# Gated half v of a gated MLP by seven products of block sums, with sums of weight blocks made in the transfers

## Chip, core and metric

The kernel runs on one core of one Trainium2 chip. The metric is the device time of one execution in microseconds (us); the profile has one execution of its own, whose span is the time from its first to its last instruction. TensorE multiplies, VectorE (DVE) and ScalarE (ACT) do elementwise work, GpSimd (POOL) a little of it, SyncE (SP) issues most transfers.

## Reference

One sample of 512 tokens with 1024 features passes two layers, each with a token mixer and a squared-ReLU MLP, all in float32. The change touches the mixer of layer 1:

```python
def spatial_gating(h, w_in, b_in, ln_g, ln_b, w_s, b_s, w_o):
    z = jax.nn.gelu(h @ w_in + b_in, approximate=False)      # w_in (1024, 6144)
    u, v = jnp.split(z, 2, axis=-1)                          # 3072 columns each
    v = layer_norm(v, ln_g, ln_b)
    v = v.reshape(bsz, n // SG_CHUNK, SG_CHUNK, SG_GROUPS, SG_GROUP_CH)
    s = jnp.einsum('gpq,bnqgc->bnpgc', w_s, v) + b_s.T[None, None, :, :, None]
    return (u * s.reshape(bsz, n, SG_HALF)) @ w_o
```

"The gated half v" is the product of h (512 x 1024) with the second 3072 columns of `w_in`, with its bias and Gelu.

## The kernel before

**Products.** Each float32 product is made of three passes in float32r: an operand is kept as a rounded part hi and a rest lo, and `products` (L183) issues hi*hi, hi*lo and lo*hi, each a matmul of 128x128 against 128x512 (or narrower). PSUM tiles come from banks named ps_mm, ps_t, ps_o and ps_s.

**Weights.** All weight pieces lie side by side in DRAM (`wall`), in the order of use. The class `Weights` streams them: SP loads a unit of 1536 columns into one of two buffers `raw` (L66), then `upto` splits it in four pieces of 384 columns, whi by a cast on ACT (L80) and wlo by a subtraction on DVE (L81). `get` asks for pieces two units ahead, so the split of a unit is issued ahead of its use. Every fourth pair of tiles lies in a pool of its own, `W.more`.

**Order.** A scheduler has put the instructions of each engine into one order; an engine runs its row strictly in that order, each instruction waiting for what it needs.

**Stages.** Layer 0 is attention and its output projection; then MLP "a". An MLP has two halves of 2048 hidden units: 16 blocks of products, each ended by `hidden` (L562 to L567: relu on ACT, square on DVE, split), then the second matrix in `residual` (L512 adds into `xall`). Between the blocks of MLP "a" stand the steps of `ada_block`, 56 in all: SP loads 512 KB into the only buffer `adaraw` (L276), and DVE reduces it (L277), one value of the modulation of layer 1 for each partition; the next load waits until DVE has read the one before.

At the end of MLP "a" the last two output blocks are done by token halves, and for each half `Norm.finish` (L156 to L159) and `modulated` (L167 to L174) make the next input, h_hi (hh) and h_lo (hl), eight chunks k of 128 features: on DVE, ACT and POOL, half 0 while PE still works on half 1.

Then comes the stage that is changed: for 6 blocks b of 512 columns and 4 tiles n of 128 tokens, 8 chunks k in three passes, 576 matmuls in all, in which tokens are the stationary operand and the weights move. A finished tile is taken from PSUM by DVE (L616, adding the bias), goes through Gelu on ACT (L617) and statistics on DVE (L618). After it the half u is computed by blocks, layer norm runs over v (L620 to L635), and L656 mixes positions.

Of the kernel before, what the change touches and what calls it, by code (L numbers as in the profile page):

```python
# [27 lines left out]
UNIT = 1536  # L28
# [9 lines left out]
# The weight stream: sections of pieces in the order of their use, (name, pieces, columns of a piece).  # L38
# [8 lines left out]

class Weights:
    """Streams of stationary or moving weight pieces, split into two float32r parts on arrival."""

    def __init__(self, nc, raw_pool, pool, wall, ahead=2):
        self.nc, self.raw_pool, self.pool, self.ahead, self.wall = nc, raw_pool, pool, ahead, wall
        self.first, self.width = {}, {}
        c = 0
        for key, n, w in SECTIONS:
            self.first[key], self.width[key] = c, w
            c += n * w
        self.tiles = {}
        self.raw = {}
        self.loaded = self.done = 0  # L60
        self.more, self.parts = None, 4
# [8 lines left out]
    def upto(self, unit):  # L70
        nc = self.nc
        while self.done <= min(unit, self.wall.shape[0] - 1):
            self.load(self.done)
            raw = self.raw.pop(self.done)
            pool = self.more if self.more is not None and self.done % 4 == 3 else self.pool
            hi = pool.tile([P, UNIT], F32R, tag="whi", name="whi")
            lo = pool.tile([P, UNIT], F32R, tag="wlo", name="wlo")
            for c in range(0, UNIT, UNIT // self.parts):
                cs = slice(c, c + UNIT // self.parts)
                nc.scalar.copy(out=hi[:, cs], in_=raw[:, cs])  # L80
                nc.vector.tensor_tensor(out=lo[:, cs], in0=raw[:, cs], in1=hi[:, cs], op=ALU.subtract)  # L81
            self.tiles[self.done] = (hi, lo)
            self.done += 1

    def get(self, key, i):
        w = self.width[key]
        u, c = divmod(self.first[key] + i * w, UNIT)
        assert c + w <= UNIT
        self.upto(u + self.ahead - 1)
        hi, lo = self.tiles[u]  # L90
# [4 lines left out]
def backbone_kernel(ctx: ExitStack, tc: tile.TileContext, x0T, xT, cols, ada0, ada1, qknorm, bias_t,  # L95
# [38 lines left out]
    h_hi = [hp.tile([P, T], F32R, tag=f"hh{k}", name=f"hh{k}") for k in range(KC)]  # L134
    h_lo = [hp.tile([P, T], F32R, tag=f"hl{k}", name=f"hl{k}") for k in range(KC)]
# [247 lines left out]
    def both(kk, j):  # L383
        """Columns of the grid keys of query block j and of the context keys, as one pattern."""
# [98 lines left out]
    W.more = ctx.enter_context(tc.tile_pool(name="wb", bufs=1, reuse_waits="tile"))  # L483
# [293 lines left out]
```

## Time and profile before

| | us |
|---|---|
| median of three runs | 1563.95 (1559.7 to 1568.19) |
| the profiled execution, its span | 1560.2 |
| PE busy | 1524.9 (98%) |
| DVE busy | 930.1 (60%) |
| ACT busy | 664.3 (43%) |
| POOL busy | 148.8 (10%) |

The profiled execution has no time of its own beside its span; the span lies within the three runs, 3.75 us below their median. Busy PE includes the time of matmuls at a lower clock. The shares are means over stages, and what a stage waits for is read from that stage.

### The profile page before, as it was taken

Reading aid. Unit: us, or ns where it says so; the run is one execution under the profiler, and the core shown is the slowest. Engines: PE = TensorE matmul, PEld = TensorE weight load, DVE = VectorE, ACT = ScalarE, POOL = GpSimd, SP = SyncE. Lnnn points to the kernel's source line nnn. Section 1 sums busy time; section 2 is a strip of 40 time slices with the busy share of each in tenths; the row PEclk is TensorE's granted clock in tenths of the full one; section 3 lists DMA queues with packets and bytes.
Section 4 is the critical chain, followed back from the end, with each engine's and each line's share of the span. In section 5 each row is a group of like instructions: output and inputs, shape, how many; then the busy total and the mean of one; then the engine's idle time right before and its main releaser. Section 6 shows DMA issues by size and latency. Waiting matters only on the chain.

```text
span 1560.2 us, 21105 instructions
## 1 busy us (share of the span) xinstructions
PE 1524.9 (98%) x7780; PEld 1287.6 (83%) x7780; DVE 930.1 (60%) x1938; ACT 664.3 (43%) x1577; POOL 148.8 (10%) x177
## 2 busy tenths in 40 slices
PE   8899999999999999999999999999999999999999
PEld 2798888887898888878988887888889988888888
DVE  5778777777776555765575468644446743334431
ACT  2566666676544322442353256423234542224320
POOL 0522222212200000000100013100001000000000
PEclk9999999999999999999999999999999999999999
DMA  9265555535146555655243225322321432223230
GB/s 354 95 171 174 164 163 167 167 113 167 62 142 211 193 193 180 202 199 179 95 128 131 91 96 176 125 92 97 106 95 41 135 109 87 96 101 102 97 112 28
DMA packets 60311, 212.06 MB, mean 136 GB/s; under 512 B 7984, under 2 KB 16816, under 8 KB 58672
## 3 DMA queue, kind: packets, MB, share of 16 engines
q1 hardware_dynamic: 48688, 200.57, 39.2%
q10 hardware_dynamic: 11520, 10.15, 2.1%
q8 instruction: 61, 1.00, 0.3%
q14 instruction: 42, 0.34, 0.1%
HBM read 193.91 MB, written 2.10 MB: 126 GB/s over the span
## 4 chain that ended last, share of the span: by engine, by line
PE 59%; DMA 8%; DVE 4%; issue 2%; ACT 1%; ACTq 0%; DVEq 0%
PE ps_mm L183 29%; PE ps_t L183 19%; PE ps_o L183 9%; DMA adaraw<-ada 8%; DVE adaraw L277 1%; PE ps_s L656 1%; DVE wlo L81 1%; DVE nt L172 1%; DVE hl L174 0%; DVE xall L512 0%; DMA raw<-wall 0%; PE ps_s L156 0%; ACT v L632 0%; DVE acc L151 0%; ACT whi L80 0%
## 5 line engine op out<-in xcount | busy, mean ns | idle before, releaser
L80 ACT CAST whi<-raw 128x384 fp32r<-128x384 f32 x620 | 278.5, 510 | 355.9 <-PE ps_mm L183 141.5
L81 DVE TENSOR_TENSOR wlo<-raw,whi 128x384 fp32r<-128x384 f32 x620 | 330.6, 581 | 144.8 <-ACT whi L80 144.6
L277 DVE CUSTOM_DVE_ANT_0 adaraw<-adaraw,cb 128x1024 f32<-128x1024 f32 x80 | 99.4, 1242 | 106.6 <-DMA adaraw<-ada 106.1
L183 PE MATMUL ps_mm<-hh,wlo 128*128 128x512 f32 (+1 forms) x416 | 154.2, 371 | 0.6 <-DVE wlo L81 0.6
L183 PE MATMUL ps_mm<-hh,whi 128*128 128x512 f32 (+1 forms) x416 | 154.4, 371 | 0.0
L183 PE MATMUL ps_mm<-hl,whi 128*128 128x512 f32 (+1 forms) x416 | 154.0, 370 | 0.0
L183 PE MATMUL ps_mm<-whi,hh 128*128 128x384 f32 (+1 forms) x352 | 124.7, 356 | 5.1 <-DVE vl L332 2.9
L183 PE MATMUL ps_mm<-wlo,hh 128*128 128x384 f32 (+1 forms) x352 | 124.8, 355 | 1.9 <-DVE wlo L81 1.9
L183 PE MATMUL ps_mm<-mh,whi 128*128 128x512 f32 (+1 forms) x336 | 122.0, 363 | 3.2 <-ACT mh L566 3.2
L183 PE MATMUL ps_mm<-whi,hl 128*128 128x384 f32 (+1 forms) x352 | 124.1, 354 | 0.0
L183 PE MATMUL ps_mm<-ml,whi 128*128 128x512 f32 (+1 forms) x336 | 122.1, 363 | 0.0
L183 PE MATMUL ps_mm<-mh,wlo 128*128 128x512 f32 (+1 forms) x336 | 121.6, 362 | 0.0
L183 PE MATMUL ps_t<-hh,whi 128*128 128x512 f32 (+1 forms) x280 | 104.5, 373 | 0.0
L183 PE MATMUL ps_t<-hl,whi 128*128 128x512 f32 (+1 forms) x280 | 104.3, 372 | 0.0
L183 PE MATMUL ps_t<-hh,wlo 128*128 128x512 f32 (+1 forms) x280 | 104.0, 371 | 0.0
L183 PEld LDWEIGHTS ps_mm<-hh,wlo 128*128 128x128 f32 x416 | 78.5, 189 | 13.8 <-DVE wlo L81 0.8
L183 PEld LDWEIGHTS ps_mm<-hh,whi 128*128 128x128 f32 x416 | 78.5, 189 | 12.6
L183 PEld LDWEIGHTS ps_mm<-hl,whi 128*128 128x128 f32 x416 | 78.6, 189 | 12.5
L566 ACT CAST mh<-relu 128x512 fp32r<-128x512 f32 x64 | 39.7, 621 | 99.0 <-DVE relu L563 99.0
L183 PEld LDWEIGHTS ps_mm<-mh,whi 128*128 128x128 f32 x336 | 64.2, 191 | 13.1 <-ACT mh L566 3.6
L183 PEld LDWEIGHTS ps_mm<-whi,hh 128*128 128x128 f32 x352 | 66.6, 189 | 10.2 <-DVE vl L332 3.2
L183 PEld LDWEIGHTS ps_mm<-wlo,hh 128*128 128x128 f32 x352 | 66.8, 190 | 7.5 <-DVE wlo L81 2.8
(204 smaller groups left out, 3322.5 us busy)
## 6 DMA issues: line engine op xcount, KB each, us to landing
raw<-wall SPq DMA_DIRECT2D x155, 768.0 KB, 4.4
adaraw<-ada SPq DMA_DIRECT2D x80, 512.0 KB, 3.9
bt<-bias_t SPq DMA_DIRECT2D x16, 512.0 KB, 3.6
aw<-ada SPq DMA_DIRECT2D x7, 1024.0 KB, 10.8
q<-th SPq DMA_DIRECT2D x32, 128.0 KB, 2.4
q<-tl SPq DMA_DIRECT2D x32, 128.0 KB, 2.3
x<-x0T SPq DMA_DIRECT2D x3, 1024.0 KB, 11.3
bc<-lngb ACTq DMA_DIRECT2D x12, 256.0 KB, 3.3
```

Source lines behind the costliest of these rows:

```text
L80: nc.scalar.copy(out=hi[:, cs], in_=raw[:, cs])
L81: nc.vector.tensor_tensor(out=lo[:, cs], in0=raw[:, cs], in1=hi[:, cs], op=ALU.subtract)
L172: vec.scalar_tensor_tensor(out=t, in0=xk, scalar=A[:, k:k + 1], in1=r, op0=ALU.mult, op1=ALU.mult)
L183: pe.matmul(o, lhsT=a, rhs=b, start=start and i == 0, stop=stop and i == n - 1)
L277: vec.tensor_tensor_reduce(out=a, in0=a, in1=cb, scale=1.0, scalar=0.0, op0=ALU.mult, op1=ALU.add, accum_out=mod[:, idx:idx + 1])
L566: act.copy(out=a, in_=r)
L656: pe.matmul(s[:, n * P:(n + 1) * P], lhsT=v[:, n, g * P:(g + 1) * P], rhs=ws, start=True, stop=True)
```

## The change

The two token halves and the two halves of the features form four blocks of h, here B11, B12 (features 0 to 511, token half 0 and 1), B21 and B22 (features 512 to 1023). A pair of column blocks of 512 and the two halves of the features form four blocks of weights, w00, w10 (first columns), w01 and w11. The plain way takes eight products of blocks; the change takes seven, of sums of blocks. It runs for three units u of 1024 columns, each with seven products of 24 matmuls (4 chunks, 2 token tiles, 3 passes), so 504 matmuls in place of 576.

What is added for it:
- Ahead of the first unit, DVE adds hh and hl again to float32 for the four blocks (f, L681), makes T1 = B11-B12, T3 = B22-B12, T2 and T4 from them (L686, L688), and ACT and DVE split each T into hi and lo (L691, L692), all as instructions of 128x1024.
- A sum of weight blocks is made by a plain load from SP (L110), and then a transfer issued by GpSimd that adds a second block (L113), each of 512 KB. The sums w01+w11 lie in two buffers `sum0` and `sum1` and are carried on: a further block is added for n6 and for n3, while n7 and n4 have sums or blocks of their own in `raw`. There are 24 such accumulating transfers, 8 in each unit, beside 10 plain loads of a unit; GpSimd issues them between its own elementwise work.
- Weights to split for this half are now 43008 columns in place of 24576, since each of the seven products has operands of its own.
- PSUM tiles are taken 14 times in a unit, 42 in all, in place of 24 (L726, L729), since a product goes into up to two outputs; Gelu and the statistics keep their 24.

Beside it: `wall` has rows of 2048 columns, `raw` is three buffers of 1024 columns in place of two of 1536, and a split piece is 512 columns in place of 384, for the whole kernel. The pool `W.more` is closed for the changed stage and opened again after it.

The core of the diff:

```diff
+PRODUCTS = (("n1", "B11"), ("n2", "B21"), ("n5", "T1"), ("n6", "T2"), ("n7", "T3"), ("n3", "B22"), ("n4", "T4"))
+def summands(blocks):
+    w00, w01, w10, w11 = blocks
+    return ((False, (w00,)), (False, (w10,)), (None, (w01, w11)), (True, (w00,)), (False, (w00, w01)),
+            (True, (w10,)), (False, (w11,)))
...
-    def load(self, unit):
-        while self.loaded <= min(unit, self.wall.shape[0] - 1):
-            raw = self.raw_pool.tile([P, UNIT], F32, tag="raw", bufs=2, name="raw")
-            self.nc.sync.dma_start(out=raw, in_=self.wall[self.loaded])
...
+            slot, go_on, what = self.stretches[self.loaded]
+            if go_on:
+                raw = self.sums[slot]
+            elif slot is None:
+                raw = self.raw_pool.tile([P, RAW], F32, tag="raw", bufs=3, name="raw")
+            else:
+                raw = self.sums[slot] = self.sum_pool.tile([P, RAW], F32, tag=f"sum{slot}", name=f"sum{slot}")
+            if not go_on:
+                self.nc.sync.dma_start(out=raw, in_=self.dram(what[0], RAW))
+                what = what[1:]
+            for c in what:
+                self.nc.gpsimd.dma_start(out=raw, in_=self.dram(c, RAW), accum_op=ALU.add)
...
-        for b in range(6):
-            w = [W.get("v", b * KC + k) for k in range(KC)]
...
-            for n in range(4):
-                ns = slice(n * P, (n + 1) * P)
-                o = mm()
-                products(o, [((h_hi[k][:, ns], h_lo[k][:, ns]), w[k]) for k in range(KC)], True, True)
-                vs = v[:, n, b * 512:(b + 1) * 512]
-                vec.tensor_tensor(out=vs, in0=o, in1=bb, op=ALU.add)
...
+            for q, (ks, ts) in quarter.items():
+                f[q] = vp.tile([P, HK, HT], F32, tag="f" + q, name="f" + q)
+                vec.tensor_tensor(out=f[q], in0=hh_all[:, ks, ts], in1=hl_all[:, ks, ts], op=ALU.add)
...
+            def operands():
+                operand("T1", f["B11"], f["B12"], False, f["B11"])
+                operand("T3", f["B22"], f["B12"], False, f["B12"])
+                operand("T2", f["B11"], f["B22"], True, f["B22"])
+                operand("T4", f["B22"], f["B21"], True, f["B21"])
...
+                X = [bank("mm", 3) for _ in range(2)]
+                Y = [bank("t", 2) for _ in range(2)]
+                Z = [bank("s", 2) for _ in range(2)]
+                into = {"n1": X, "n2": Y, "n5": Z, "n6": X, "n7": X, "n3": Z, "n4": X}
+                for j, (name, q) in enumerate(PRODUCTS):
+                    hi, lo = ops[q]
+                    o = into[name]
+                    for k in range(HK):
+                        w = W.get("v", (u * 7 + j) * HK + k)
+                        for i in range(2):
+                            ts = slice(i * P, (i + 1) * P)
+                            products(o[i], [((hi[:, k, ts], lo[:, k, ts]), w)],
...
```

Three places of the order follow, in which the names carry the numbers of their buffers. The first is DVE's row where the norm of token half 1 ends (hl is its last result). Before, evacuations of PSUM (L616) and statistics (L618) stand between the parts of hl, and weights (L81) behind:

```order
L172 SCALAR_TENSOR_TENSOR nt_7803<-xall_4516,A1_1_83,rstd_7774 128x256 [waits DVE_49]
L618 BN_STATS st1_7819<-v_7817 128x6 [waits Activation_49]
L174 SCALAR_TENSOR_TENSOR hl6_101<-nt_7803,mod_80,hh6_93 128x256 [waits Activation_49]
L170 TENSOR_TENSOR hl7_102<-nt_7807,hh7_94 128x256 [waits Activation_49]
L616 TENSOR_TENSOR v_7817<-ps_t_7918,bc_7860 128x512 [waits PE_49]
L618 BN_STATS st2_7820<-v_7817 128x6 [waits Activation_49]
L81 TENSOR_TENSOR wlo_7977<-raw_7974,whi_7976 128x384 [waits DMAHW2_49,Activation_49]
```

Now the operands stand there, and ahead of them nothing of the stage v; the first sum's wlo and n1's evacuations stand among them:

```order
L681 TENSOR_TENSOR fB22_7760<-hh_87,hl_88 128x1024 [waits DVE_49]
L688 TENSOR_TENSOR fB11_7754<-fB11_7754,fB12_7756 128x1024 [waits DVE_49]
L729 TENSOR_TENSOR v_7744<-ps_mm_7785,bb_7782 128x512 [waits DMAHW3_49,PE_49]
L688 TENSOR_TENSOR fB12_7756<-fB22_7760,fB12_7756 128x1024 [waits DVE_49]
L692 TENSOR_TENSOR T1l_7764<-fB11_7754,T1h_7763 128x1024 [waits Activation_49]
L686 SCALAR_TENSOR_TENSOR fB22_7760<-fB11_7754,fB22_7760 128x1024 [waits DVE_49]
L692 TENSOR_TENSOR T3l_7769<-fB12_7756,T3h_7768 128x1024 [waits Activation_49]
L686 SCALAR_TENSOR_TENSOR fB21_7758<-fB22_7760,fB21_7758 128x1024 [waits DVE_49]
L692 TENSOR_TENSOR T2l_7774<-fB22_7760,T2h_7773 128x1024 [waits Activation_49,Pool_49]
L124 TENSOR_TENSOR wlo_7822<-sum0_7827,whi_7821 128x512 [waits DMASW2_49]
L692 TENSOR_TENSOR T4l_7779<-fB21_7758,T4h_7778 128x1024 [waits Activation_49]
L729 TENSOR_TENSOR v_7744<-ps_mm_7786,bb_7782 128x512 [waits PE_49]
```

Ahead of the first of these twelve stand, behind the last hl, fB11, fB12 and fB21; behind the last stand the other three pieces of wlo for n5. So eleven instructions of 128x1024 and one evacuation stand between the last hl and the piece of wlo for n5's first chunk or among its follow-ups.

The second place is PE's row after the first 48 matmuls of the stage. Before, the third token tile of the first column block stands there, whose operands are those of half 1's norm:

```order
L183 MATMUL ps_t_7918<-whi_7512,hh0_87 128x512 [waits Activation_49]
L183 MATMUL ps_t_7918<-wlo_7513,hh0_87 128x512
L183 MATMUL ps_t_7918<-whi_7512,hl0_95 128x512 [waits DVE_49]
L183 MATMUL ps_t_7918<-whi_7512,hh1_88 128x512 [waits Activation_49]
L183 MATMUL ps_t_7918<-wlo_7513,hh1_88 128x512
```

Now n5 stands there, behind n1 and n2, which use token half 0 alone; its operands are T1 and the first sum:

```order
L239 MATMUL ps_s_7789<-whi_7821,T1h_7763 128x512 [waits Activation_49]
L239 MATMUL ps_s_7790<-whi_7821,T1h_7763 128x512
L239 MATMUL ps_s_7789<-wlo_7822,T1h_7763 128x512 [waits DVE_49]
L239 MATMUL ps_s_7789<-whi_7821,T1l_7764 128x512
L239 MATMUL ps_s_7790<-wlo_7822,T1h_7763 128x512
L239 MATMUL ps_s_7790<-whi_7821,T1l_7764 128x512
L239 MATMUL ps_s_7789<-whi_7852,T1h_7763 128x512 [waits Activation_49]
L239 MATMUL ps_s_7789<-wlo_7853,T1h_7763 128x512 [waits DVE_49]
```

The third place is DVE's row within a unit: before, splits of loaded weights and evacuations alternate:

```order
L81 TENSOR_TENSOR wlo_7989<-raw_7986,whi_7988 128x384 [waits DMAHW7_49,Activation_49]
L81 TENSOR_TENSOR wlo_7989<-raw_7986,whi_7988 128x384 [waits Activation_49]
L616 TENSOR_TENSOR v_7817<-ps_o_7946,bc_7860 128x512 [waits PE_49]
L81 TENSOR_TENSOR wlo_7989<-raw_7986,whi_7988 128x384 [waits Activation_49] x2
L618 BN_STATS st3_7821<-v_7817 128x6 [waits Activation_49]
```

Now, in the first unit, the split of a sum that waits for an accumulating transfer (the semaphores DMASW) stands ahead of the two evacuations of n6, which free the banks that n7 uses next; and that transfer itself waits for the splits that read the same buffer for n6:

```order
L124 TENSOR_TENSOR wlo_7918<-raw_7921,whi_7917 128x512 [waits Activation_49]
L124 TENSOR_TENSOR wlo_7950<-raw_7946,whi_7949 128x512 [waits DMASW1_49,DVE_49,Activation_49]
L124 TENSOR_TENSOR wlo_7950<-raw_7946,whi_7949 128x512 [waits Activation_49]
L124 TENSOR_TENSOR wlo_7950<-sum0_7827,whi_7949 128x512 [waits DMASW6_49,Activation_49]
L729 TENSOR_TENSOR v_7744<-ps_mm_7785,bb_7782 128x512 [waits PE_49]
L729 TENSOR_TENSOR v_7744<-ps_mm_7786,bb_7782 128x512 [waits PE_49]
```

In the second unit the splits of both sums for n3 stand ahead of n6's evacuations. One thing moves outside of the stage: in MLP "a", counting the steps of `ada_block` in DVE's row, the square for the last hidden block of its second half now stands behind the 74th of them, before behind the 71st.

## Rows read from the trace of the kernel before

**Rows 1.** The page: busy us (share of the span) and instructions

```profile
PE 1524.9 (98%) x7780; PEld 1287.6 (83%) x7780; DVE 930.1 (60%) x1938; ACT 664.3 (43%) x1577; POOL 148.8 (10%) x177
```

**Rows 2.** The page's chain that ended last, by line

```profile
PE ps_mm L183 29%; PE ps_t L183 19%; PE ps_o L183 9%; DMA adaraw<-ada 8%; DVE adaraw L277 1%; PE ps_s L656 1%; DVE wlo L81 1%; DVE nt L172 1%; DVE hl L174 0%; DVE xall L512 0%; DMA raw<-wall 0%; PE ps_s L156 0%; ACT v L632 0%; DVE acc L151 0%; ACT whi L80 0%
```

**Rows 3.** Timeline of PE: start us, us, what, [idle before <-releaser]

```profile
700.30 0.80 PE L183 MATMUL ps_mm<-mh,whi 128*128 128x512 f32 x1 [3.17 <-ACT mh L566]
...
782.37 0.40 PE L183 MATMUL ps_mm<-whi,hh 128*128 128x512 f32 x1
...
786.50 0.70 PE L156 MATMUL ps_s<-acc,ones 128*128 128x256 f32 x2 [1.00 <-DVE acc L151]
...
914.69 0.39 PE L183 MATMUL ps_mm<-hh,whi 128*128 128x512 f32 x1
```

**Rows 4.** Windows: us, busy (x) by engine, PEclk, DMA share, GB/s

```profile
850.00:860.00 10.00, 10.00 (x46) 8.29 (x45) 4.77 (x9) 3.02 (x6) 0.00 (x0) 1.00 0.69 249
790.00:915.00 125.00, 125.00 (x553) 103.55 (x552) 66.46 (x122) 46.34 (x95) 2.39 (x3) 1.00 0.32 103
```

**Rows 5.** Timeline of DVE at the norm of token half 1

```profile
787.81 1.75 DVE L159 RECIPROCAL rstd<-rstd 128x256 f32<-128x256 f32 x1
...
791.17 0.68 DVE L616 TENSOR_TENSOR v<-ps_mm,bc 128x512 f32<-128x512 f32 x1
...
798.76 0.42 DVE L170 TENSOR_TENSOR hl<-nt,hh 128x256 fp32r<-128x256 f32 x1
```

**Rows 6.** Lines by shape: busy us, mean ns, idle before

```profile
L81 DVE TENSOR_TENSOR wlo<-raw,whi 128x384 fp32r<-128x384 f32 x620 | 330.6, 581 | 144.8 <-ACT whi L80 144.6
...
L566 ACT CAST mh<-relu 128x512 fp32r<-128x512 f32 x64 | 39.7, 621 | 99.0 <-DVE relu L563 99.0
...
L169 ACT CAST hh<-nt 128x256 fp32r<-128x256 f32 x18 | 7.0, 389 | 0.0
```

**Rows 7.** Instructions of L634: duration ns min/median/max

```profile
L634 DVE TENSOR_TENSOR v<-v,bc x12: 1211/1224/3022, 921.1 to 983.7; 128x1024 f32<-128x1024 f32 x12
```

**Rows 8.** Windows after PE's wait for mh, columns as in group 4

```profile
700.00:705.00 5.00, 4.70 (x10) 3.43 (x11) 2.19 (x4) 1.90 (x5) 0.00 (x0) 0.50 0.43 144
705.00:710.00 5.00, 5.00 (x20) 4.04 (x19) 3.42 (x9) 0.00 (x0) 0.00 (x0) 0.85 0.76 234
710.00:715.00 5.00, 5.00 (x24) 4.14 (x23) 2.30 (x5) 2.28 (x5) 0.00 (x0) 1.00 0.37 138
```

**Rows 9.** Timeline of DVE: two steps of ada_block

```profile
449.70 1.22 DVE L277 CUSTOM_DVE_ANT_0 adaraw<-adaraw,cb 128x1024 f32<-128x1024 f32 x1
...
697.76 1.22 DVE L277 CUSTOM_DVE_ANT_0 adaraw<-adaraw,cb 128x1024 f32<-128x1024 f32 x1 [0.64 <-DMA adaraw<-ada]
```

**Rows 10.** DMA issues: tile, queue, count, KB each, median us to landing

```profile
raw<-wall SPq DMA_DIRECT2D x155, 768.0 KB, 4.4
adaraw<-ada SPq DMA_DIRECT2D x80, 512.0 KB, 3.9
...
xall<-xT SPq DMA_DIRECT2D x2, 1024.0 KB, 6.5
```

**Rows 11.** Transfers into adaraw

```profile
DMA to landing us min/median/max: 3.3/3.9/10.2
```

**Rows 12.** Timelines of DVE and POOL after the stage v

```profile
926.33 1.49 DVE L662 TENSOR_TENSOR u<-u,gt 128x512 f32<-128x512 f32 x1
...
929.13 0.69 DVE L662 TENSOR_TENSOR u<-u,gt 128x512 f32<-128x512 f32 x1
...
932.23 2.73 DVE L81 TENSOR_TENSOR wlo<-raw,whi 128x384 fp32r<-128x384 f32 x1
...
924.90 2.37 POOL L635 TENSOR_TENSOR v<-v,bc 128x1024 f32<-128x1024 f32 x1 [127.61 <-PE ps_s L656]
```

**Rows 13.** Timeline of DVE: the last evacuation of v

```profile
915.36 0.68 DVE L616 TENSOR_TENSOR v<-ps_mm,bc 128x512 f32<-128x512 f32 x1
```

**Rows 14.** Matmuls of L656: ns min/median/max, first and last start

```profile
L656 PE MATMUL ps_s<-ws,v x192: 270/275/347, 924.4 to 1169.8; 128*128 128x128 f32 x192
```

More of the change, by code (lines that the diff above doesn't have):

```diff
@@ L27 @@
 EPS = 1e-6
-UNIT = 1536
+UNIT = 2048
+RAW = 1024
+PART = 512
+HILO = 1536
 KOFF = (0, 1, 3, 4)
@@ L57, in __init__, with dram @@
             c += n * w
-        self.tiles = {}
-        self.raw = {}
+        self.raw, self.tiles, self.sums = {}, {}, {}
         self.loaded = self.done = 0
-        self.more, self.parts = None, 4
-    def load(self, unit):
-        while self.loaded <= min(unit, self.wall.shape[0] - 1):
-            raw = self.raw_pool.tile([P, UNIT], F32, tag="raw", bufs=2, name="raw")
-            self.nc.sync.dma_start(out=raw, in_=self.wall[self.loaded])
+        self.more = self.sum_pool = None
+    def dram(self, c, n):
+        u, c = divmod(c, UNIT)
+        assert c + n <= UNIT
+        return self.wall[u][:, c:c + n]
@@ L67, in load, with pair @@
             self.raw[self.loaded] = raw
             self.loaded += 1
-    def upto(self, unit):
-        nc = self.nc
-        while self.done <= min(unit, self.wall.shape[0] - 1):
-            self.load(self.done)
[L74 to L82, printed above, removed]
+    def pair(self, n):
+        pool = self.more if self.more is not None and n % 4 == 3 else self.pool
+        return (pool.tile([P, HILO], F32R, tag="whi", name="whi"),
+                pool.tile([P, HILO], F32R, tag="wlo", name="wlo"))
@@ new lines, in split, with upto @@
+    def split(self, src, hi, lo):
+        self.nc.scalar.copy(out=hi, in_=src)
+        self.nc.vector.tensor_tensor(out=lo, in0=src, in1=hi, op=ALU.subtract)
+    def upto(self, part):
+        while self.done <= min(part, len(self.stretches) * RAW // PART - 1):
+            self.load(self.done)
+            t, c = divmod(self.done * PART, HILO)
+            if t not in self.tiles:
+                self.tiles[t] = self.pair(t)
+            hi, lo = self.tiles[t]
+            r, rc = divmod(self.done * PART, RAW)
+            self.split(self.raw[r][:, rc:rc + PART], hi[:, c:c + PART], lo[:, c:c + PART])
@@ L83, in upto @@
             self.done += 1
+            if self.done * PART % RAW == 0:
+                del self.raw[r]
     def get(self, key, i):
         w = self.width[key]
[L87 to L90, printed above, removed]
+        t, c = divmod(self.first[key] + i * w, HILO)
+        assert c + w <= HILO
+        self.upto((t + self.ahead) * (HILO // PART) - 1)
+        hi, lo = self.tiles[t]
         return hi[:, c:c + w], lo[:, c:c + w]
@@ L132, in mvec @@
         return mod[:, i:i + KC]
[L134 to L135 removed]
+    hh_all = hp.tile([P, KC, T], F32R, name="hh")
+    hl_all = hp.tile([P, KC, T], F32R, name="hl")
+    h_hi = [hh_all[:, k] for k in range(KC)]
+    h_lo = [hl_all[:, k] for k in range(KC)]
     class Norm:
@@ L176, in backbone_kernel, with products @@
     HALVES = ((0, T // 2), (T // 2, T))
-    def products(o, terms, start, stop):
+    def products(o, terms, start, stop, shared=False):
         n = len(terms) * 3
@@ L182, in products @@
             for a, b in ((ah, bh), (ah, bl), (al, bh)):
-                pe.matmul(o, lhsT=a, rhs=b, start=start and i == 0, stop=stop and i == n - 1)
+                pe.matmul(o, lhsT=a, rhs=b, start=start and i == 0, stop=stop and i == n - 1,
+                          skip_group_check=shared)
                 i += 1
```

98 lines of the change are left out of this document (87 added, 11 removed).

## Prediction, made before the changed kernel ran

> **What bounds the kernel now.** I read the page's first part first: PE is busy 98% of the span, the other engines 60% and less [rows 1]. The chain that ended last agrees: its large shares are matmuls, and the one other item of size is the load into `adaraw` with the DVE step that reads it [rows 2]. So fewer matmuls give time only where nothing makes PE wait in their place. Then I read the stage itself. It lasts from PE's first matmul of v at 782.37 to the first of u at 914.69 [rows 3], 132.3 us; from 790 to 915 PE is busy all the time, 553 matmuls in 125.00 us, 0.226 us each, at full clock, while DVE works 66.5 of it and ACT 46.3 [rows 4]. 576 matmuls of 0.226 are 130.2 us, and the other 2.1 us are the norm of token half 1 (its matmul, 1.00 us idle before it [rows 3]). The stage is bound by PE alone, with its DVE half idle.
>
> **The matmuls that go.** 72 x 0.226 = 16.3 us, in full clock. This is what there is to gain.
>
> **The operands T.** n1 and n2 use token half 0 and can run at once: 48 x 0.226 + 2.1 = 13.0 us, to 795.3; without a wait n5 would end 5.4 us later, at 800.8. But n5 needs T1, which needs both token halves. On DVE the norm of half 1 runs from 787.81 to 799.18; between its parts stood the evacuation at 791.17 and three more instructions of v of its size [rows 5], which now come later, so the last hl ends some 3 us sooner, near 796. Behind it DVE has eleven instructions of 128x1024 and one evacuation before or among the wlo pieces of n5. A product of 128x1024 took 1.21 to 1.22 us at the minimum and median [rows 7], 1.2 with the overlap of neighbours; the evacuation 0.68 [rows 5], 0.65 in a row. Four f and T1 end at 796 + 5 x 1.2 = 802.0. T1's cast on ACT is a little over 1 us (256 columns took 0.389 and 512 columns 0.621 [rows 6], an estimate of 0.23 for each further 256 gives 1.07), and two matmuls of n5 can go near 803. The third waits for wlo of n5's first chunk, which stands behind one evacuation and six more of 1.2: 802.0 + 7.2 + 0.65 = 809.9, and 0.6 for itself (a piece of 384 took 0.58 [rows 6]): 810.5. T4l, an evacuation and a second piece make 813.0, the two others 813.6 and 814.2. From the second piece, 18 matmuls remain: 813.0 + 18 x 0.226 = 817.1.
>
> PE has then been all but idle for some 15 us. What the clock does after an idle stretch, the end of the hidden stage shows: after 3.17 us without work at 700.30 [rows 3], the granted clock was 0.50 for 5 us and 0.85 for the next 5, and 54 matmuls ran up to 715, where 14.7 us hold 65 at full clock: 2.5 us lost [rows 8]. 0.50 is the 1.2 GHz level. I put 2 us here, since a part of that slow time falls into the waits for pieces. n5 ends near 819: **18.2 us lost**, which is more than the whole gain. Bounds: 15 if the clock stays up and the DVE pitch is 1.15; 22 if DVE is slowed beside GpSimd. For that the trace has L662 with 1.49 us beside a POOL instruction and 0.69 without, and a wlo piece with 2.73 in place of 0.58 [rows 6, 12]; two transfers are issued by GpSimd in that stretch, +2.2 each at the worst. I take no such slowing, since the POOL instruction there is a 2.4 us pass over 1024 columns [rows 12] and an issue moves no data through DVE's side that any row shows.
>
> **The accumulating transfers.** The trace of before has none. Nearest are plain loads of the same 512 KB, 3.3 at the least, 3.9 in the median and 10.2 at the most [rows 11], and one of 1024 KB with 6.5 [rows 10]. They go in pairs (sum0 and sum1), with plain loads beside, so 1024 KB is the nearest in bytes: I take L = 6 us from issue to landing, bounds 3.3 to 10.2. They start late by construction: a sum for n6 or n3 can only be added to when the splits of the sum before are read, so between two products that share a buffer lies L and nothing can be fetched ahead. For n5's own sums the cover is the T chain: the plain load lands and the addition follows the POOL parts of the norm near 797, landing by 803 at L = 6, before 809.9. For n6 of the first unit the additions start when n5's pieces are split, 810.5 and 814, and are wanted when n5 ends at 819; with L = 6 the second is some 1 us late (split and cast after landing). For n3 the wait stands on DVE ahead of n6's evacuations, which n7 needs, and PE's first five matmuls of n3 stand ahead of n7: +2.4; in the other two units the same row holds n6's evacuations, +1 together. Sum **+4 at L = 6**, 0 at 3.3, and +24.5 at 10.2 (three units with two exposed waits each of about 4).
>
> The Trainium skill ("DMA: Bandwidth & Descriptors", section "Anatomy of one DMA — SWDGE (gpsimd) path") gives a fit of 2.0 us plus bytes over 436 KB/us for a transfer issued by GpSimd, from which an estimate of 3.2 us for 512 KB follows, near the lower bound; the sum would then end 4 us lower, and no row here shows it or an accumulation.
>
> **DMA engines, DVE and ACT in a unit.** 18 transfers of 512 KB are 9.4 MB in 168 x 0.226 = 38 us, 248 GB/s. The trace moved 249 GB/s from 850 to 860 at a share of 0.69 with PE never idle [rows 4], so plain loads at this rate hide. DVE has per unit 28 pieces of 0.7, 14 evacuations of 0.68 and 8 statistics of 0.69, some 30 of 38 us; ACT some 20. All of it lies beside PE, price 0; should DVE's cover go (a wait of 5 us at the head of its row), its slack of 8 us pays first.
>
> **The end of v.** Last evacuation 915.36 [rows 13], first matmul of L656 at 924.4 [rows 14], 9.1 us of norm that u's products covered; 51 of them now stand there, 11.5 us, against a chain of about 10 to 11.5 with the pools reopened. +0.5 (0 to 1).
>
> **MLP "a".** The steps of `ada_block` run as one chain, load then DVE: the step at 449.70 to that at 697.76 is 46 periods, 5.39 us each [rows 9], and the last one made PE wait 3.17 us, plus the 2.5 us of clock, 5.7. Now 49 periods come ahead of that block. At an unchanged 5.39 that is 3 x 5.39 = +16; at 248.1/49 = 5.06 nothing changes; at (248.1 - 5.7)/49 = 4.95 the wait goes, -5.7. The load beside it now has 512 KB in place of 768, and the row puts one to four DVE instructions between the split that frees `raw` and the step, so the two overlap less; a load alone took 3.3, with 1.22 for the step 4.6 a period [rows 9, 11]. I take 0 between these ends. Coarser pieces and smaller `raw` elsewhere: PE is the bound there, 0.
>
> **Sum.** -16.3 + 18.2 + 4 + 0.5 + 0 = +6.4, on the profiled 1560.2: 1566.6. That execution lies 3.75 under the median of the three runs, so against the median the forecast is **1570 us**, +0.4%, by about 0.5% (7.8 us) what a measurement of this kernel can tell from no change.
>
> **Rivals.**
> - A, faster: the T stall is at its lower bound, the accumulations land in 3.3 us and the ada chain falls under 4.95: 1570.3 - 3.2 - 4 - 5.7 = 1557; a shorter T stall than 15 would need DVE to be ahead of the norm, which its row excludes. Decides at a period of 5.0.
> - B, slower: the accumulation is the bound. With L at 10.2 it is 1570 + 20.5 = 1591. If the addition takes engine time for reading the destination too, 8 of 18 transfers count twice, 13.6 MB in 38 us or 358 GB/s, at the row's 249 GB/s for 0.69 [rows 4] just 0.99 of the engines; counted three times, 17.8 MB need 49 us, +11 in each unit, 1570 + 33 = 1603. It decides from L of about 7 on. Against it: nothing in the trace of before; for it: the buffer is shared in place, so no wait can be fetched ahead.
> - By the same page of the Trainium skill (sections "Issuing engines are not separate DMA queues" and "Rules for kernel authors") all transfers run on the same 16 engines, and an accumulation reads its destination and writes it later; by that rule B would be the case, and no row here shows it.
> - C, slower: the ada chain keeps 5.39: 1570 + 16 = 1586.
> - D: n5's stall is covered by work that PE does instead. PE's row has none to offer: n5 stands next in it. 1552; a chance of a few per cent.
>
> **Chances.** Forecast 0.48, A and D 0.17, B 0.20, C 0.15. Of the forecast's cases some two thirds lie within 7.8 us of the median and a third above; A lies mostly within or just beyond. Faster 0.12, same 0.40, slower 0.48. The range for 8 in 10 leaves out the worst of B and the best of D: 1556 to 1594; the forecast's own is 1563 to 1578.
>
> **What would show it.** Right: one long idle of PE in n5, ended by DVE (T or wlo), 12 to 16 us long near 796 to 814, half clock after it; the stage from first v to first u matmul near 138 us; accumulating transfers with a landing near 6; PE waits on wlo in n6 or n3 of a few us. The steps fall if DVE's twelve instructions end before 806, if landings lie above 8, if the period of `ada_block` differs from 5.06 by over 0.1, or if PE waits elsewhere than in v.

## The result, and the profile after

The changed kernel took 1615.5 us in the median of four runs (1612.15 to 1615.96), the kernel before 1564.16: a ratio of 1.031, 95% interval 1.027 to 1.035, so 51 us slower in the medians and above the whole range. The sections below go by the two profiled executions, which differ by 50.2 us. The profiled execution has a span of 1610.4. First the page of the changed kernel, its engines, two of its DMA queues (packets, MB, share of 16 engines) and two of its DMA issues; it answers to [rows 1, 10]:

```profile
PE 1527.2 (95%) x7708; PEld 1283.4 (80%) x7708; DVE 956.9 (59%) x1848; ACT 673.9 (42%) x1461; POOL 167.9 (10%) x201
...
q1 hardware_dynamic: 60640, 203.45, 39.8%
q0 software_dynamic: 3456, 12.58, 4.4%
...
raw<-wall SPq DMA_DIRECT2D x232, 512.0 KB, 4.4
...
sum<-wall POOLq DMA_DIRECT2D x18, 512.0 KB, 7.0
```

PE is busy as long as before, with 72 matmuls fewer; what came is idle time, and matmuls at a lower clock. PE's timeline of the changed kernel, at the places where it stood (answers to [rows 3]):

```profile
714.53 0.79 PE L239 MATMUL ps_mm<-mh,whi 128*128 128x512 f32 x1 [4.75 <-ACT mh L629]
...
796.63 0.40 PE L239 MATMUL ps_mm<-whi,hh 128*128 128x512 f32 x1
...
818.90 1.22 PE L239 MATMUL ps_s<-whi,T1h 128*128 128x512 f32 x2 [9.28 <-ACT whi L123]
...
825.36 0.80 PE L239 MATMUL ps_s<-wlo,T1h 128*128 128x512 f32 x1 [5.24 <-DVE wlo L124]
...
861.95 0.51 PE L239 MATMUL ps_mm<-whi,hh 128*128 128x512 f32 x1 [2.00 <-DVE v L726]
...
879.76 0.50 PE L239 MATMUL ps_mm<-whi,T2h 128*128 128x512 f32 x1 [2.01 <-ACT whi L123]
...
895.92 0.80 PE L239 MATMUL ps_mm<-whi,T3h 128*128 128x512 f32 x1 [6.27 <-DVE v L729]
...
960.39 0.39 PE L239 MATMUL ps_mm<-hh,whi 128*128 128x512 f32 x1
...
1006.90 0.49 PE L239 MATMUL ps_mm<-gh,whi 128*128 128x512 f32 x1 [4.31 <-ACT gh L802]
```

Stage v runs from 796.63 to 960.39, 163.8 us in place of 132.3. With the first norm matmul of the attention's output as a further mark (414.98 before, 422.50 after), the 50.2 us of the two profiles fall apart so: 7.5 ahead of that norm, 6.7 from there to stage v (MLP "a"), 31.4 in stage v, and 4.5 after it, where a wait for gh takes 4.31 us that took 0.83 before.

Within stage v, by its units (the first one parted behind n5; windows of the changed kernel, columns as in [rows 4]):

```profile
796.63:833.00 36.37, 20.68 (x76) 15.10 (x74) 31.74 (x44) 15.56 (x27) 6.94 (x9) 0.77 0.65 141
833.00:858.88 25.88, 23.21 (x96) 17.80 (x97) 19.65 (x32) 13.14 (x24) 3.43 (x4) 1.00 0.88 213
858.88:914.53 55.65, 44.36 (x170) 34.35 (x168) 32.45 (x53) 21.30 (x39) 6.90 (x8) 0.88 0.80 196
914.53:960.39 45.86, 41.13 (x169) 32.45 (x168) 30.92 (x53) 20.23 (x36) 5.20 (x6) 0.96 0.71 175
```

504 matmuls at 0.226 and the norm's 2.1 us would be 116. n5 ended at 833.0, 36.4 us after the stage's start, where 18.5 were needed: 17.9 lost. The rest of the first unit lost 4.2, the second unit 17.7 (55.65 for 38.0) and the third 7.9. The granted clock was 0.77 and 0.88 in the two parts with long waits, so a share of their loss is matmuls at a lower clock behind a wait (how large a share is not worked out here). In the second unit PE waited 6.27 us for an evacuation (L729) and twice 2 us, for an evacuation and a cast. DVE's row around n5 (answers to [rows 5, 7]):

```profile
811.49 4.62 DVE L681 TENSOR_TENSOR fB<-hh,hl 128x1024 f32<-128x1024 f32 x4
816.03 1.22 DVE L688 TENSOR_TENSOR fB<-fB,fB 128x1024 f32<-128x1024 f32 x1
817.21 0.69 DVE L729 TENSOR_TENSOR v<-ps_mm,bb 128x512 f32<-128x512 f32 x1
...
823.49 1.22 DVE L692 TENSOR_TENSOR T2l<-fB,T2h 128x1024 fp32r<-128x1024 f32 x1
824.62 0.69 DVE L124 TENSOR_TENSOR wlo<-sum,whi 128x512 fp32r<-128x512 f32 x1
825.23 1.22 DVE L692 TENSOR_TENSOR T4l<-fB,T4h 128x1024 fp32r<-128x1024 f32 x1
826.36 0.68 DVE L729 TENSOR_TENSOR v<-ps_mm,bb 128x512 f32<-128x512 f32 x1
826.96 1.88 DVE L124 TENSOR_TENSOR wlo<-sum,whi 128x512 fp32r<-128x512 f32 x3
```

The operands stand there as the order said, 1.13 to 1.18 us from the start of one to that of the next; wlo for n5's first chunk starts at 824.62, behind T2l, and n5 goes on at 825.36. And the DMA queues in the second unit, 858 to 915, with the share of 16 engines of the accumulating queue (q0) and the plain one (q1):

```profile
q0 software_dynamic: 1320, 4.76, 45.9%
q1 hardware_dynamic: 1635, 5.97, 31.8%
```

45.9% of 57 us for 4.76 MB is 5.50 us of all 16 engines per MB; 31.8% for 5.97 MB is 3.04. So a byte that is added took 1.8 times the engine time of a byte that is loaded plainly.

### The profile page after: what moved, and what is told of

Same layout as the page of the kernel before. It is cut to its first block, busy times and chain, and to the rows that moved or that the text cites. A ratio compares the mean times of both kernels' runs of the same rounds, so it can differ in the third digit from the quotient of the medians.

```text
span 1610.4 us, 21082 instructions
## 1 busy us (share of the span) xinstructions
PE 1527.2 (95%) x7708; PEld 1283.4 (80%) x7708; DVE 956.9 (59%) x1848; ACT 673.9 (42%) x1461; POOL 167.9 (10%) x201
## 3 DMA queue, kind: packets, MB, share of 16 engines
q0 software_dynamic: 3456, 12.58, 4.4%
## 4 chain that ended last, share of the span: by engine, by line
PE 67%; DMA 14%; DVE 10%; issue 4%; ACT 3%; POOL 1%; ACTq 0%; DVEq 0%; SPq 0%; POOLq 0%
PE ps_mm L239 33%; PE ps_t L239 17%; PE ps_o L239 11%; DMA adaraw<-ada 7%; DMA raw<-wall 3%; DMA sum<-wall 3%; DVE wlo L124 3%; PE ps_t L496 2%; DVE adaraw L334 1%; PE ps_s L793 1%; ACT whi L123 1%; PE ps_s L458 1%; DMA kgain<-qknorm 1%; PE ps_s L459 1%; DVE nt L228 1%
## 5 line engine op out<-in xcount | busy, mean ns | idle before, releaser
L123 ACT CAST whi<-raw 128x512 fp32r<-128x512 f32 x464 | 264.5, 619 | 392.1 <-PE ps_mm L239 152.7
L124 DVE TENSOR_TENSOR wlo<-raw,whi 128x512 fp32r<-128x512 f32 x464 | 320.9, 727 | 153.8 <-ACT whi L123 153.5
L239 PE MATMUL ps_mm<-whi,hh 128*128 128x384 f32 (+1 forms) x280 | 97.9, 351 | 8.2 <-DVE vl L389 3.2
L239 PE MATMUL ps_mm<-wlo,hh 128*128 128x384 f32 (+1 forms) x280 | 96.7, 346 | 0.2 <-DVE wlo L124 0.2
L239 PE MATMUL ps_mm<-whi,hl 128*128 128x384 f32 (+1 forms) x280 | 96.3, 346 | 0.0
L239 PEld LDWEIGHTS ps_mm<-hh,wlo 128*128 128x128 f32 x416 | 78.3, 188 | 13.7 <-DVE wlo L124 0.8
L239 PEld LDWEIGHTS ps_mm<-ml,whi 128*128 128x128 f32 x336 | 64.1, 191 | 13.5 <-DVE ml L630 3.9
L568 DVE SCALAR_TENSOR_TENSOR xall<-ps_mm,mod,xall 128x512 f32<-128x512 f32 (+1 forms) x47 | 30.7, 656 | 70.7 <-PE ps_mm L239 70.7
```

What stands on the lines that cost most here:

```text
L123: self.nc.scalar.copy(out=hi, in_=src)
L124: self.nc.vector.tensor_tensor(out=lo, in0=src, in1=hi, op=ALU.subtract)
L568: vec.scalar_tensor_tensor(out=x[m][:, c0:c1], in0=o[:, c0:c1], scalar=gate(m), in1=x[m][:, c0:c1], op0=ALU.mult, op1=ALU.add)
```

## Experiments

Each kernel was profiled once, so a row is one execution, not a median. How far single profiles differ is seen in the first two rows, which are the same kernel: 2.7 us in the attention, 4.5 in MLP "a", nothing in stage v. p1's profile is the slowest of its four runs, which spread over 18 us. e2, e3, i1, d1, e6 and h4 leave a part of the work out, to price it. Stages in us, from the first matmul of each mark: up to the first norm; to stage v; stage v; the rest; span.

| kernel | attention | MLP a | stage v | rest | span |
|---|---|---|---|---|---|
| before | 415.0 | 367.4 | 132.3 | 645.5 | 1560.2 |
| b0, before again | 417.7 | 362.9 | 132.3 | 647.1 | 1560.0 |
| changed | 422.5 | 374.1 | 163.8 | 650.0 | 1610.4 |
| e1_grain | 421.5 | 372.0 | 133.0 | 646.1 | 1572.5 |
| g0_pools | 419.3 | 368.1 | 133.4 | 646.6 | 1567.4 |
| g1_part512 | 413.2 | 364.8 | 133.5 | 651.5 | 1562.9 |
| e2_plain | 419.8 | 372.6 | 134.2 | 650.7 | 1577.3 |
| i1_inplace_sync | 425.9 | 373.6 | 145.8 | 649.7 | 1595.0 |
| e3_overwrite | 424.1 | 372.0 | 147.2 | 650.7 | 1594.0 |
| d1_fewer_loads | 422.7 | 371.9 | 150.4 | 649.9 | 1594.9 |
| e6_no_t | 421.2 | 377.9 | 152.0 | 650.6 | 1601.8 |
| o1_order | 418.1 | 375.1 | 159.0 | 650.3 | 1602.5 |
| x1_ada2_after | 422.6 | 369.0 | 166.5 | 650.3 | 1608.4 |
| h4_hybrid_no_add | 420.8 | 368.7 | 130.5 | 648.1 | 1568.1 |
| p1_pool_sums | 424.3 | 371.4 | 150.2 | 650.9 | 1596.8 |
| h3_hybrid | 421.9 | 368.5 | 151.8 | 649.8 | 1592.0 |
| x2_ada2_before | 419.6 | 366.2 | 132.3 | 645.5 | 1563.6 |
| x4_part512_ada2 | 414.2 | 362.3 | 133.6 | 649.5 | 1559.6 |

**What the sums cost: four kernels with the T chain and all 504 matmuls.** e2_plain, e3_overwrite and i1_inplace_sync differ from the changed kernel in a line each:

```diff
 e2: -  self.stretches.append((slot, go_on, [b + h * RAW for b in what]))
     +  self.stretches.append((None, False, [what[0] + h * RAW]))
 e3: -  self.nc.gpsimd.dma_start(out=raw, in_=self.dram(c, RAW), accum_op=ALU.add)
     +  self.nc.gpsimd.dma_start(out=raw, in_=self.dram(c, RAW))
 i1: +  self.nc.sync.dma_start(out=raw, in_=self.dram(c, RAW))
```

> The changed kernel without any addition of weight blocks: each of the seven products of a unit loads one plain block through raw from SyncE (its result is not the product; additions of weight blocks are left out). T operands, 504 matmuls, splits and evacuations stay. Theory: the transfers that add in place cost 29 us of the stage (4 in the first unit, 17.5 and 8 in the others), so stage v falls from 163.8 to about 134 to 137 us and the span to about 1582. Rival: splits, evacuations and their order on VectorE are what makes the later units slow; then stage v stays above 150 and the span above 1597.

> The changed kernel with each of the 24 GpSimd transfers writing its block over the buffer instead of adding it (additions left out); same bytes, same buffers, same order and waits on every engine. Theory 1: the time is in the in-place order (one buffer pair, issue by GpSimd after the last reader, nothing fetched ahead), so landing stays near 6 to 7 us and the span within 6 us of 1610. Theory 2: the adding itself is slow (it reads its destination); then landing falls from 7.0 to about 4 and the stage by 15 us or more, span 1590 to 1597.

> The changed kernel with each of the 24 additions made a plain write over the same buffer from SyncE (nothing is added; GpSimd issues nothing). Theory: most of the 13 us between e3_overwrite (stage v 147.2) and e2_plain (134.2) is the rewriting of one pair of buffers, which waits for its readers: stage v 144 or more. Rival: GpSimd as issuer (0.86 us an issue in its row, landing 4.8 us in place of 4.4 to 5.0) is what costs: stage v 138 or less.

Stage v is 134.2 with one plain load for each product and half, into the three buffers of the stream; 145.8 when the changed kernel's 24 further blocks are written in place by SyncE, 147.2 by GpSimd, and 163.8 when they are added. So the adding itself is worth 16.5 us (e3 has the changed kernel's order on every engine), GpSimd as issuer 1.4, and the rewriting in place 11.6. The last of these has more in it than the one pair of buffers: e2 loads 42 tiles in the stage and i1 54, and no run parts those 12 from the rewriting. Of e3's two theories neither holds alone: the time fell as theory 2 said, but 13 us stayed. The 24 adding transfers of the changed kernel (L113), from issue to landing:

```profile
DMA to landing us min/median/max: 5.4/7.6/11.2
```

The same 24 transfers in e3_overwrite, which add nothing, with its GpSimd queue, whose 2.5% of 1594 us for 12.58 MB are 3.2 us per MB, a plain load's rate (the changed kernel's 4.4% of 1610 are 5.6):

```profile
DMA to landing us min/median/max: 3.9/5.1/9.1
...
q0 software_dynamic: 3456, 12.58, 2.5%
```

In i1 PE waits at the start of the second and third unit for evacuations of n4 (L726); in DVE's row splits stand ahead of them whose raw comes late, 4.40 us late on ACT. On SP that load is queued behind writes to the sums, which wait for their readers:

```profile
862.24 0.66 PE L239 MATMUL ps_mm<-whi,hh 128*128 128x512 f32 x1 [2.04 <-DVE v L726]
...
905.76 0.50 PE L239 MATMUL ps_mm<-whi,hh 128*128 128x512 f32 x1 [2.46 <-DVE v L726]
...
856.87 0.62 ACT L123 CAST whi<-raw 128x512 fp32r<-128x512 f32 x1 [4.40 <-DMA raw<-wall]
```

**Are the DMA engines full, or is it the order?** d1_fewer_loads lets n1, n2 and n4 of the second and third unit split a tile that is in SBUF (`slot = f"f{h}"` in place of a load), so that 12 plain loads go; o1_order moves products:

```diff
-PRODUCTS order in every unit: n1 n2 n5 n6 n7 n3 n4
+ORDERS = (n1 n2 n5 n6 n7 n3 n4, n1 n5 n2 n6 n7 n3 n4, n1 n5 n2 n6 n7 n3 n4)
```

> The changed kernel, in whose second and third unit the products n1, n2 and n4 split a tile that is in SBUF already in place of a loaded block (those 12 plain loads of 512 KB are left out, and the result is not the product). All 24 accumulating transfers, matmuls, splits and evacuations stay. Theory: the DMA engines' time is the bound of these units: at 5.5 us of 16 engines per MB for accumulating and 3.04 for plain loads a unit needs 41 us against 38 of PE; without 3.1 MB of plain loads it needs 32, so the two units fall from 101.5 us together to 84 or less. Rival: the additions in place, one after the other, are the bound; then they stay above 94.

> The changed kernel with the products of its second and third unit in the order n1, n5, n2, n6, n7, n3, n4, so that one other product lies between those whose sums are made in place of one another; first unit, bytes, transfers and arithmetic stay. Theory: the 25 us that these two units lose come from n6's addition following right on the reading of n5's sum, with 7 us of landing against 5.4 us of cover; they fall to at most 10, span 1594 or less. Rival: it is the number of transfers in flight, or DVE's rows; then less than 6 us come back, span 1604 or more.

The two units of d1, columns as before:

```profile
857.20:905.75 48.55, 41.74 (x170) 33.03 (x168) 31.44 (x52) 20.35 (x37) 6.91 (x8) 0.89 0.79 168
905.75:944.98 39.23, 38.69 (x169) 31.48 (x168) 30.94 (x53) 19.83 (x35) 3.46 (x4) 1.00 0.49 114
```

87.8 us in place of 101.5: between the two bounds, 13.7 of the 25.6 us that these units lost, so those loads beside the sums are worth about half of the loss there; the rest may be the additions in place. The third unit is near its 38 us at a DMA share of 0.49. o1 brought back 4.7 us of stage v, the rival's number: with more cover the sums only landed later, 8.3 us in the median of its 24 adding transfers in place of 7.6. That the engines had no room is argued from the share of the two queues, 84% of this unit, 848 to 905:

```profile
q0 software_dynamic: 1390, 5.10, 50.3%
q1 hardware_dynamic: 1759, 6.38, 33.8%
...
sum<-wall POOLq DMA_DIRECT2D x8, 512.0 KB, 8.9
```

**T alone.** e6_no_t puts blocks of h in T's place:

```diff
-            operands()
+            ops.update(T1=ops["B12"], T2=ops["B22"], T3=ops["B12"], T4=ops["B21"])
```

> The changed kernel without the operands T: n5, n6, n7 and n4 take blocks of h as they are (the sums of token blocks and their splits are left out). Weight sums, transfers and evacuations stay. Theory: n5's stall of 18 us is VectorE's chain of eleven 1024-column instructions; it shrinks to what the first sum leaves, at most 3, and the span falls by 15 to 18 to 1592 to 1595. Rival: n5 waits for the sum's landing anyhow (its first wait was ended by the cast of the sum); then the span falls by less than 9, above 1601.

Stage v fell by 11.7, the span by 8.6, since MLP "a" was 3.8 us longer in this profile. Without T, n5 waits for the cast of the first sum, and ends 7.5 us late:

```profile
815.68 0.80 PE L239 MATMUL ps_s<-whi,hh 128*128 128x512 f32 x1 [4.25 <-ACT whi L123]
```

Without the sums (e2) it ended 13.6 us late, with both 17.9: the two stalls lie in part on top of each other, and the span fell as the rival said.

**The stretch ahead of stage v.** e1_grain is the changed kernel with eight products as before; g0_pools has only the moved pools (rows of 1536, two buffers, splits of 384), g1_part512 as g0 with splits of 512.

```diff
 e1: UNIT = 2048, RAW = 1024, PART = 512, three raw buffers
 g0: UNIT = 1536, RAW = 1536, PART = 384, two raw buffers
 g1: UNIT = 1536, RAW = 1536, PART = 512, two raw buffers
```

> The changed kernel with the gated half v computed as before (six column blocks, eight products, no block sums, no GpSimd transfers); the 2048-column rows of the wall, raw buffers of 1024 columns, splits of 512 columns and the moved pools stay, and every engine's order ahead of v is that of the changed kernel. Theory: of the 50 us, 14 us arise ahead of v from the coarser weight stream and pools alone, so first v matmul near 796.6 (before 782.4), stage v 132 us, span 1574 to 1579. Rival: the stretch ahead of v was slow by chance or through the seven products; then first v near 782 and span near 1560.

> The kernel before with the moved pools of the change (W.more, the norm's tiles, the output projection's pools, hh and hl as one tile each) and nothing else: rows of 1536 columns, two raw buffers, splits of 384. Theory: the 12 to 14 us ahead of stage v come from the weight stream's new sizes, so this runs as before: first v matmul near 782 to 784, span 1558 to 1564. Rival: the pools cost them; then span 1570 or more.

> As g0_pools, but splits of 512 columns in place of 384 (rows and raw buffers of 1536 columns stay). If the coarser split is what costs (a cast of 512 holds ScalarE 0.62 us in place of 0.51 between the steps of the attention's softmax): span 1569 to 1574, with PE's wait for pb near 9 us. If the loads of 512 KB in three buffers are what costs: span 1558 to 1564.

> The kernel before, profiled once more as a measure of what one profile differs from another by stage. If 415 us to the first norm (attention) and 367 from there to stage v come again within 2 us, then the 421 and 374 of the kernels with the new weight stream are theirs; if they spread over 415 to 421, the 6 us of the attention are chance.

e1 has 12.3 of the 50 us without any seven products, 11.1 of them ahead of stage v. The pools alone show 7 in their one profile, 4 of them in the attention, where the kernel before differs from itself by as much (415.0, 417.7, and 419.6 with x2's order, which is the same there); the split of 512 costs nothing. What is left, as far as it is not chance, is the loads of 1024 columns, with their three buffers and longer rows, which are not taken apart. The changed kernel in the attention: one of ACT's waits, and the group of its splits from 65 to 415 us; the last row is that group in h4_hybrid_no_add (below), which has before's loads and splits there:

```profile
189.24 0.62 ACT L123 CAST whi<-raw 128x512 fp32r<-128x512 f32 x1 [1.80 <-DMA raw<-wall]
...
L123 ACT CAST whi<-raw 128x512 fp32r<-128x512 f32 x59 | 33.8, 625 | 22.6 <-DMA raw<-wall 12.7 <-PE ps_mm L239 9.8
...
L140 ACT CAST whi<-raw 128x384 fp32r<-128x384 f32 x80 | 36.8, 513 | 10.5 <-PE ps_mm L254 10.4
```

ACT waits 12.7 us for raw, with the softmax's exponentials queued behind; PE waits 9.4 for them (pb). e1 has the same 12.7 and 9.6; in before, b0, g0 and g1 that wait for raw is 0.3 at most. So the waits are the new stream's. What they cost is not shown. The mean of the nine kernels with this stream is 422.0 for the attention, of three profiles with before's order 417.4; but h3, h4 and p1, with before's loads and splits here and none of these waits, have 421.9, 420.8 and 424.3. All profiles without the new stream lie between 413 and 424, those with it between 418 and 426, so that 5 us of this stretch may be chance.

**MLP "a".** x1_ada2_after and x2_ada2_before give every other step of `ada_block` a tile of its own:

```diff
-                            ada_block(nxt)
+                            ada_block(nxt, sp if nxt % 2 else None)
```

> The changed kernel with a second tile for the loads of ada_block in MLP a (every other one), no other change. Theory: the 6.7 us that MLP a lost are the chain load, step, load through one buffer, at 5.19 us a period for 49 periods; with two buffers the waits for mh and ml (7.7 us together) and the half clock after them go, so from the first norm to stage v 374 becomes 364 to 367, span 1600 to 1604. Rival: splits and raw loads of the new sizes hold MLP a; then 371 or more.

> The kernel before with the same second tile. Theory: its one wait of 3.2 us and the half clock behind it go: from the first norm to stage v 367 (363 in its second profile) becomes 361 to 363, ratio to before 0.995 to 0.998. Rival: the waits move into the next load, ratio 0.999 to 1.001.

The chain in the changed kernel, the 25th and the 74th step on DVE (answers to [rows 9]):

```profile
457.58 1.22 DVE L334 CUSTOM_DVE_ANT_0 adaraw<-adaraw,cb 128x1024 f32<-128x1024 f32 x1
...
711.99 1.23 DVE L334 CUSTOM_DVE_ANT_0 adaraw<-adaraw,cb 128x1024 f32<-128x1024 f32 x1 [1.19 <-DMA adaraw<-ada]
```

49 periods in 254.4 us, 5.19 each. x1 took out the 4.75 us wait at 714.53 and 5.1 us of the stretch (369.0), two short of the theory, since two waits grew earlier, where the second matrix of the first half begins (the changed kernel has 0.71 and 0.65 us there):

```profile
532.97 0.50 PE L239 MATMUL ps_mm<-mh,whi 128*128 128x512 f32 x1 [1.20 <-ACT mh L629]
...
536.18 0.79 PE L239 MATMUL ps_mm<-ml,whi 128*128 128x512 f32 x1 [2.71 <-DVE ml L630]
```

x2 does the same to the kernel before. Its 3.17 us went, and another wait came, 170 us earlier:

```profile
531.34 0.56 PE L183 MATMUL ps_mm<-ml,whi 128*128 128x512 f32 x1 [3.47 <-DVE ml L567]
```

Ratio 0.999 (0.997 to 1.002): the rival's.

**Versions.** h3_hybrid computes the first pair of column blocks by eight products, with T made beside it, and keeps before's stream outside the stage; h4 leaves its additions out, p1 lets GpSimd add; x4 is g1 with x2's second tile.

```diff
 h3: +ORDERS = (None, n1 n5 n2 n6 n7 n3 n4, n1 n5 n2 n6 n7 n3 n4); WIDE = 1536, CUT = 384 outside v
 h4: -self.add(None if go_on is False else h, go_on, [b + h * RAW for b in of], RAW, PART)
     +self.add(None, False, [of[0] + h * RAW], RAW, PART)
 p1: +self.nc.sync.dma_start(out=more, in_=self.dram(c, width))
     +self.nc.gpsimd.tensor_tensor(out=raw, in0=raw, in1=more, op=ALU.add)
```

> A version meant to keep what works: the weight stream of before outside stage v (1536 columns, splits of 384), the first pair of column blocks by eight products as before, with the operands T made beside it, and the other two pairs by seven products in the order of o1_order. 528 matmuls in place of 576, 16 accumulating transfers. Theory (T chain, in-place sums and stream are all of the loss): 48 x 0.226 = 10.9 us less than before, with 0 to 5 given back by sums: profile span 1549 to 1555, ratio 0.993 to 0.997. Rival (accumulating transfers cost wherever they stand): no faster than before, ratio 0.998 or more.

> h3_hybrid without any addition of weight blocks (each sum is one plain block, additions left out). Theory: with T's chain under the plain unit and no accumulating transfer nothing of the loss in stage v is left: stage v 132.3 - 10.9 = 121.4, at most 123. Rival: the seven products have another cost (evacuations of 14 tiles in a unit, T's instructions beside PE), stage v above 126.

> h3_hybrid with the sums made by GpSimd itself: SyncE loads each summand into a spare tile (as many bytes, none accumulating), and GpSimd adds it to the sum, 128x1024, 8 times a unit. DMA engines then need 9.4 MB x 3.04 = 29 us of 38. Theory: stage v near 121 to 127 and a ratio to before of 0.993 to 1.0. Rival: GpSimd's 2.4 us additions and VectorE hold each other up (L662 took 1.49 in place of 0.69 us beside one), 8 x 2.4 us beside a VectorE that has 31 of 38 us to do: stage v above 130, ratio above 1.0.

> The kernel before with the pools of the change, splits of 512 columns (as g1_part512) and the second tile for ada_block; eight products in stage v. If g1's shorter attention (413 us to the first norm) was not chance, it runs 3 to 8 us below before: ratio 0.995 to 0.998; if it was, ratio 0.998 to 1.001.

h3 is slower than before, 1.015 (1.013 to 1.017): stage v 151.8, 21.3 above h4, which leaves the sums out. h4 has 130.5, 1.8 less than before and 9 above the theory: 2.6 in the plain unit, 2.2 and 4.1 in the others, where n7 stands right behind n6 in the banks and waits 1.3 and 0.9 us for its evacuations; the rest of these is not taken apart. So in this form seven products gain 1.8 us of stage v before any sum is paid. p1 is at 1.015 too (1.011 to 1.019). The pieces of wlo on DVE in p1, and an addition on GpSimd:

```profile
L146 DVE TENSOR_TENSOR wlo<-raw,whi 128x512 fp32r<-128x512 f32 x30 | 35.4, 1209 | 9.5 <-ACT whi L145 9.2
L146 DVE TENSOR_TENSOR wlo<-sum,whi 128x512 fp32r<-128x512 f32 x23 | 21.4, 957 | 3.0 <-ACT whi L145 3.0
...
L135 POOL TENSOR_TENSOR sum<-sum,fB 128x1024 f32<-128x1024 f32 x10 | 26.1, 2606 | 40.6 <-DVE wlo L146 26.5 <-DMA sum<-wall 11.6 <-issue 2.5
```

The same piece in h4, with no additions:

```profile
L141 DVE TENSOR_TENSOR wlo<-raw,whi 128x512 fp32r<-128x512 f32 x54 | 35.1, 686 | 16.9 <-ACT whi L140 16.9
```

1.21 and 0.96 us in place of 0.69. GpSimd's passes hold DVE up, as L662 in [rows 12]: in p1's timeline the 11 pieces of wlo<-raw that run beside an addition took 2.12 us in the mean, the 18 others 0.68. DVE is busy 83.6 of 97 us of the two units. x4 is at 1.000 (0.998 to 1.003). No kernel here beats the one before.

## Why the prediction was wrong

The forecast was 1570 us in the median, +6.4 us on the profiled time; it came to 1615.5, and +50.2 on the profile. By the forecast's terms the 50.2 are -16.3 for the matmuls, +18.2 for what e2 lost without any sum, +29.6 for the sums, and 18.7 outside of stage v.

- **The matmuls that go, -16.3: right.** The second and third unit of e2 took 39.4 and 38.7 us, where 168 x 0.226 is 38.0.
- **The T stall, 18.2: right in size, in part by luck.** n5 ended 36.4 us after the stage's start, forecast 36.6. The chain began 1.2 us later than I had it (a part of the norm on GpSimd came late) and ran in 1.14 us steps in place of 1.2; the two offset each other. The first sum has a part in it: without T it alone makes 7.5, and without sums n5 is 13.6 late. That e2's stage lost just 18.2 is chance as well: 13.6 of it lie at n5 and 4.6 behind it.
- **The sums, +4: this step failed.** They measured 29.6 (163.8 against e2's 134.2). The forecast let the two later units pay "+1 together" at a landing of L = 6; the adding transfers landed in 7.6 in the median and 11.2 at the most, and three things met: the adding (16.5 us), the rewriting in place with 12 more transfers (11.6), GpSimd as issuer (1.4). The paragraph on DMA engines is where it went wrong: it priced 9.4 MB a unit at a plain load's share and put 0. With 5.50 and 3.04 us per MB a unit needs 4.19 x 5.50 + 5.24 x 3.04 = 39 us, and the bias loads about 2 more, against 38 of PE. d1, which took 12 plain loads away, gave back 13.7 of the 25.6 us of two units.
- **Rival B** named this mechanism and its point ("8 of 18 transfers count twice", 0.99 of the engines; "from L of about 7 on"), with a chance of 0.20; its times of 1591 to 1603 were without the 11.6 us of rewriting and the 18.7 us outside of stage v. The Trainium skill's rule in "DMA: Bandwidth & Descriptors" ("Rules for kernel authors"), that an accumulation reads its destination and writes it later, would have had me double the bytes. The trace agrees with 1.8 times the engine time, though no run shows the reading itself. The Trainium skill's fit on the same page ("Anatomy of one DMA — SWDGE (gpsimd) path"), from which an estimate of 3.2 us came for a landing, is not reached beside other transfers: 5.4 us at the least with adding, 3.9 with plain writes in e3.
- **MLP "a", 0 between -5.7 and +16: mis-sized.** It measured +6.7 against the profile that the forecast used (before itself differs by 4.5 in this stretch). The period fell to 5.19, not 5.06: 49 x 0.13 = 6.4, over the 0.1 that the forecast named as a sign. x1 shows the chain as the cause of most of it, 5.1.
- **Elsewhere, 0: open.** It measured 7.5 in the attention. "PE is the bound there" overlooked ACT's row: smaller loads land too late for the split, the softmax stands behind it, and PE waits 9.4 us for pb. Whether that costs the span anything stays open, since h3, h4 and p1 are as long there without these waits.
- **The end of v, +0.5: too low**, 4.5. e1 and e2 differ in the products of stage v and have 646.1 and 650.7 in that stretch, and PE's wait for gh is 1.9 us in e1, 4.2 in e2 and 4.3 in the changed kernel. But h4 has 648.1 without that wait, and g1 and x4, with eight products, have 651.5 and 649.5. What makes it stays open.

## What to carry to other kernels

Price an accumulating transfer as its own kind: multiply engine time per byte by what a row shows (here 1.8) and set the sum against the stage's PE time before asking how long one lands. A stage bound by PE with idle DVE and DMA is no free room for a scheme that trades matmuls for sums: here 16.3 us of matmuls bought 18 us of waiting for operands at the one place where PE had nothing else, and transfers that needed 41 us of the engines for 38 of PE. A buffer that is added to in place cannot be fetched ahead; count what waits behind its reader on each in-order row. Change the grain of a stream by itself first, as it moves waits in stages that the change never names, and profile more than once before a few us of such a stage are put down to it.

## What was not expected of the hardware

Adding in a transfer cost 5.50 us of 16 engines per MB against 3.04 for a plain load beside it, while the same bytes written plainly by GpSimd cost 3.2, about a plain load's rate. An issue of an adding transfer held GpSimd's row for 0.86 us in the median, that of the same transfer without adding 0.53 (e3). A wlo piece of 128x512 on DVE took 2.12 us in the mean where it ran beside one of GpSimd's additions and 0.68 where it did not (p1); those additions took 2.6 us.
